# All right-hand SBUF pools moved down by 128 bytes: where weights and moving operands lie modulo 256

## The chip, the cores and the metric

The kernel runs on one core of one Trainium2 chip. The metric is the device time of that core in microseconds. The time before is the median of three runs, 2258.73 us (2254.85 to 2258.97). Beside it there is one profiled execution, whose trace all rows here come from.

## The reference, cut to what matters

One residual decoder block over a sequence of 2048 positions with 1024 channels, all in float32. The normalized and modulated input `h` is multiplied by a wide weight `w_in` (1024 x 8192). Its columns feed a recurrent branch and a branch of windowed attention; both are projected, gated, merged and projected once more.

```python
h = rms_norm(x, g_norm[l]) * (1.0 + scale[:, None, :]) + shift[:, None, :]
proj = h @ w_in[l]
x_rnn, z_rnn, q, k, v, z_attn, g_r, g_a = jnp.split(proj, IN_SPLITS, axis=-1)
...
y_rnn = (hr * jax.nn.silu(z_rnn.astype(jnp.float32))).astype(dt) @ w_out_rnn[l]
...
y_attn = (o * jax.nn.silu(z_attn.astype(jnp.float32))).astype(dt) @ w_out_attn[l]
...
merged = jax.nn.sigmoid(g_r + bg_r) * y_rnn + jax.nn.sigmoid(g_a + bg_a) * y_attn
x = x + gate[:, None, :] * (merged @ w_o[l])
return rms_norm(x, g_final)
```

## The kernel before, in words

**Precision.** Every large product is made of three matmuls of type float32r: each operand is split into a high and a low part, and `mm3` (line 151) issues high x high, high x low and low x high into one accumulator. In a matmul the *weights* (`lhsT`, 128 x 128) are loaded into the array by a weight load, and the *moving operand* (the right operand, 128 x up to 512) streams past them. The weight load of the next matmul runs while a matmul streams.

**Block products.** The products of `h` with the columns of `w_in` (other than the value columns) are done in seven block multiplications instead of eight for each pair of column blocks (`strassen`, line 348). One block multiplication is one call of `prod`: four slices `k` with three matmuls each, twelve matmuls of 512 columns. The weights are the S tiles (`s_tile`, line 190): a ring of seven tiles S0 to S6 of 4096 bytes per partition, each with the high part of four 128 x 128 blocks and then the low part. The moving operands are the tiles T (`slot`, line 485), of 8192 bytes per partition, four slices of 2048 bytes; they hold blocks of `h` and sums of them, named B11, B21, B22, T1 to T4. The kernel runs over the sequence in two halves `f`. In the first, S is made on the core: raw columns are loaded by SyncE's queue into the R tiles, ScalarE makes the high part and GpSimd the low part (`split_s`, line 207), and each S is also stored to memory. In the second half the S tiles are loaded back (`load_next`, line 312). Outputs go to the PSUM tiles X, Y, Z, W and V.

**Value products.** Ahead of the block products of each half stands `values` (line 797). Here the roles are turned: S moves, 256 columns at a time, and slices of T, or of the tile b12 (line 553), are the weights.

**Attention and output products.** Then comes the attention stage. Between its steps a generator (`steps`) issues the output products `pj`: weights in S0 to S3 again (`load_wd`, line 335), moving operands `yh` and `yl` (`split_y`, line 1688). The last stage multiplies by `w_o` into `pq`, with the weights `mh`, `ml` and the moving operands `oh`, `ol`.

**Where the tiles lie.** On-chip memory is filled from two sides in each partition. The left side grows upward, the right side downward from byte 229,344. `pS`, `pR`, `wS` and `wq` are opened on the right in this order, and after `wS` and `wq` are closed `fl` takes their place. The left side holds the pool `hp` of the T tiles, `vx` with b12, and later `ap` and `fp`. All sizes here are multiples of 32 bytes, and a slice of 128 float32 values is 512 bytes. The start addresses in the kernel before, in bytes within a partition, are:

| tile | pool, side | start | modulo 256 | modulo 512 |
|---|---|---|---|---|
| S0 to S3 | pS, right | 212,960 + 4096 i | 224 | 480 |
| S4, S5, S6 | wS, right | 192,480; 196,576; 200,672 | 224 | 480 |
| yh; yl | fl, right | 159,712 + 2048 i; 178,144 + 2048 i | 224 | 480 |
| T | hp, left | 18,528 + 8192 i | 96 | 96 |
| b12 high, low, first half | vx, left | 149,248; 157,440 | 0 | 256 |
| b12 high, low, second half | vx, left | 141,536; 149,728 | 224 | 224 |
| oh; ol | fp, left | 18,528; 51,296 | 96 | 96 |
| mh; ml | fp, left | 108,640 + 4096 i; 120,928 + 4096 i | 96 | 96 |

The pool `vx` is opened twice, and b12 lies in another place in each half. Every slice of S, T, yh, yl, oh, ol, mh, ml and b12 begins at a multiple of 512 bytes behind the start of its tile.

The pools and the helper of the change stand in this part of the kernel:

Of the kernel before, what the change touches and what calls it, by code (L numbers as in the profile page):

```python
# [10 lines left out]
F32 = mybir.dt.float32  # L11
# [9 lines left out]
P = 128  # L21
# [68 lines left out]
def decoder_block(ctx, tc, x, c, positions, g_norm, w_mod, b_mod, w_in, b_gate, conv_w, conv_b,  # L90
# [4 lines left out]
    def T(pool, shape, dt, tag, **kw):  # L95
        cnt[0] += 1
        return pool.tile(shape, dt, tag=tag, name=f"{tag}_{cnt[0]}", **kw)
# [388 lines left out]
        return T(hp, [P, KH, CH], F32R, "T", bufs=14)  # L486


    pS = pools.open("pS", side="right", bufs=1)
    pR = pools.open("pR", side="right", bufs=1)  # L490
    wS = pools.open("wS", side="right", bufs=1)
# [1403 lines left out]
```

## Time and profile before

| | |
|---|---|
| median of three runs | 2258.73 us (2254.85 to 2258.97) |
| span of the profiled execution | 2256.2 us |
| TensorE busy | 2212.2 us, 98% of the span |
| share of TensorE in the chain that ended last | 58% |
| mean granted TensorE clock | 0.992 |
| read from memory, written to it | 357.44 MB, 213.91 MB |

The profiled execution's own time is known by its span, 2256.2 us, which lies inside the spread of the three runs. The stages by the span: start and first values to 138 us, block products of the first half to 700 us, values of the second half to 813 us, its block products to 1386 us, attention with most of the output products to about 2005 us, and the rest of these with the last stage to the end.

How to read the rows: a row of the timeline gives the start in us, the time from the first start to the last end, the engine, the line and operation, the output and inputs by the program's names, the shape and the number of instructions merged. Line 149 is `mm`, the helper that issues every matmul, so the tiles tell matmuls apart. The end of a matmul is modelled and reaches into the next one; the starts are measured, and the spacing of matmuls is the difference of starts.

### The profile page before, as it was taken

How to read it: one execution, taken by the hardware profiler on the slowest of the kernel's cores; microseconds unless marked ns; L12 is line 12 of the kernel's file. 1: busy time of each engine (PE TensorE's matmuls, PEld its weight loads, DVE VectorE, ACT ScalarE, POOL GpSimd, SP SyncE). 2: the span in 40 equal slices, each digit the busy share in tenths (PEclk: the TensorE clock that was granted, in tenths of full speed). 3: DMA queues.
4: the chain of work that ended last, by engine and by line, in shares of the span. 5: the costliest groups of instructions: out<-in, count | busy, mean ns of one | idle time of the engine just before them, and what ended most of it. 6: DMA issues, size and time to landing. Idle time of an engine off the chain costs nothing.

```text
span 2256.2 us, 33998 instructions
## 1 busy us (share of the span) xinstructions
PE 2212.2 (98%) x11422; PEld 1856.8 (82%) x11422; DVE 1346.9 (60%) x2380; ACT 1257.3 (56%) x2481; POOL 977.8 (43%) x734
## 2 busy tenths in 40 slices
PE   8999999999999999999999999999999998999998
PEld 5988888888878988888888877888889887978887
DVE  5838877778555815444445343566667877666443
ACT  6638668668543627556546302677778887533211
POOL 2457676767557422222223102455566655332100
PEclk9999999999999999999999999999999999999999
DMA  8367887887998378888888988988888897899442
GB/s 286 115 219 255 281 290 260 291 277 262 326 277 292 110 235 267 278 279 272 283 280 278 332 291 277 287 252 256 263 269 262 241 264 217 255 329 285 153 132 89
DMA packets 428626, 573.64 MB, mean 254 GB/s; under 512 B 72134, under 2 KB 292514, under 8 KB 427428
## 3 DMA queue, kind: packets, MB, share of 16 engines
q1 hardware_dynamic: 390612, 451.73, 64.9%
q10 hardware_dynamic: 37648, 119.70, 13.8%
q8 instruction: 90, 1.47, 0.3%
q14 instruction: 84, 0.69, 0.1%
q0 software_dynamic: 192, 0.05, 0.0%
HBM read 357.44 MB, written 213.91 MB: 253 GB/s over the span
## 4 chain that ended last, share of the span: by engine, by line
PE 58%; DMA 4%; DVE 2%; issue 2%; ACT 2%; POOL 2%; SPq 1%; ACTq 0%; POOLq 0%; DVEq 0%
PE pj L149 11%; PE X L149 9%; PE V L149 8%; PE pq L149 8%; PE Z L149 4%; PE W L149 4%; PE sc L149 4%; PE Y L149 4%; PE o L149 4%; DMA vraw<-vN 1%; PE pT L1498 1%; PE pg L149 1%; DMA meT<-fg 1%; PE pT L1511 1%; DMA kraw<-qT 1%
## 5 line engine op out<-in xcount | busy, mean ns | idle before, releaser
L149 PE MATMUL pj<-yh,S 128*128 128x512 f32 x1024 | 370.0, 405 | 10.5 <-ACT yh L157 4.6
L149 PE MATMUL V<-T,S 128*128 128x512 f32 x1344 | 330.8, 395 | 1.7 <-DVE t L450 1.7
L149 PE MATMUL X<-T,S 128*128 128x512 f32 x1344 | 331.3, 395 | 0.9 <-POOL S L163 0.9
L163 POOL TENSOR_TENSOR S<-R,S 128x512 fp32r<-128x512 f32 x168 | 253.5, 1516 | 171.6 <-ACT S L157 70.3
L149 PEld LDWEIGHTS V<-T,S 128*128 128x128 f32 x1344 | 252.6, 188 | 61.9 <-DVE t L450 2.3
L149 PEld LDWEIGHTS X<-T,S 128*128 128x128 f32 x1344 | 252.4, 188 | 61.2 <-POOL S L163 1.7
L149 PEld LDWEIGHTS pj<-yh,S 128*128 128x128 f32 x1024 | 194.3, 190 | 49.4 <-ACT yh L157 6.1
L149 PE MATMUL pj<-yl,S 128*128 128x512 f32 x512 | 202.9, 396 | 6.1 <-POOL yl L163 5.1
L1414 ACT ACTIVATE pp<-pp,st 128x256 f32<-128x256 f32 (+3 forms) x256 | 133.8, 524 | 95.8 <-DVE st L1413 94.8
L163 POOL TENSOR_TENSOR S<-s,S 128x512 fp32r<-128x512 f32 x84 | 128.6, 1531 | 121.7 <-ACT S L157 77.8
L149 PE MATMUL Z<-T,S 128*128 128x512 f32 x672 | 165.8, 395 | 0.0
L149 PE MATMUL Y<-T,S 128*128 128x512 f32 x672 | 165.7, 395 | 0.0
L149 PE MATMUL W<-T,S 128*128 128x512 f32 x672 | 165.4, 395 | 0.0
L149 PEld LDWEIGHTS W<-T,S 128*128 128x128 f32 x672 | 126.3, 188 | 30.1 <-issue 0.9
L149 PEld LDWEIGHTS Z<-T,S 128*128 128x128 f32 x672 | 126.3, 188 | 29.4
L149 PEld LDWEIGHTS Y<-T,S 128*128 128x128 f32 x672 | 126.4, 188 | 29.2
L166 DVE TENSOR_TENSOR ptl<-pT,pth 128x384 fp32r<-128x384 f32 (+1 forms) x160 | 97.9, 628 | 75.6 <-ACT pth L157 73.4
L163 POOL TENSOR_TENSOR s<-R,s 128x512 fp32r<-128x512 f32 x32 | 46.5, 1452 | 204.9 <-ACT s L157 201.8
L157 ACT ACTIVATE S<-R 128x512 fp32r<-128x512 f32 x168 | 101.8, 622 | 47.4 <-DMA R<-in_w_in_dram 21.6
L905 DVE SCALAR_TENSOR_TENSOR xc<-xr,par,xc 128x512 f32<-128x512 f32 x96 | 95.6, 996 | 47.3 <-ACT xc L899 45.0
L1478 ACT ACTIVATE pp<-pp,M 128x256 f32<-128x256 f32 (+3 forms) x256 | 117.9, 522 | 10.0 <-DVE M L1601 10.0
L1413 DVE CUSTOM_DVE_ANT_0 pp<-sc,msk 128x256 f32<-128x256 f32 (+3 forms) x256 | 104.7, 449 | 24.6 <-PE sc L149 22.1
(334 smaller groups left out, 4729.9 us busy)
## 6 DMA issues: line engine op xcount, KB each, us to landing
sD<-S ACTq DMA_DIRECT2D x196, 512.0 KB, 4.1
S<-sD SPq DMA_DIRECT2D x196, 512.0 KB, 4.9
S<-wD SPq DMA_DIRECT2D x100, 512.0 KB, 5.7
R<-in_w_in_dram SPq DMA_DIRECT2D x136, 256.0 KB, 4.3
wD<-s ACTq DMA_DIRECT2D x64, 256.0 KB, 5.1
T<-in_w_mod_dram SPq DMA_DIRECT2D x8, 1024.0 KB, 12.0
vN<-ev SPq DMA_DIRECT2D x64, 128.0 KB, 2.8
zaT<-ev SPq DMA_DIRECT2D x32, 256.0 KB, 4.1
```

The costliest lines, as they stand in the source:

```text
L149: nc.tensor.matmul(o, lhsT=l, rhs=r, start=st, stop=sp, **kw)
L157: nc.scalar.activation(o, i, AF.Copy)
L163: nc.gpsimd.tensor_tensor(o, i, h.bitcast(F32), ALU.subtract)
L166: return nc.vector.tensor_tensor(o, i, h.bitcast(F32), ALU.subtract).ins
L905: nc.vector.scalar_tensor_tensor(xc, xr[:, i : i + CH], cw(i), xc, ALU.mult, ALU.add)
L1413: nc.vector.tensor_tensor_reduce(pdst, s_ps, mask, 1.0, 3e38, ALU.add, ALU.min, m_)
L1414: nc.scalar.activation(pdst, pdst, AF.Exp, bias=m_, scale=-1.0, accum_out=l_)
L1478: nc.scalar.activation(pp, pp, AF.Copy, scale=w)
L1498: nc.tensor.transpose(pt[:, c0 + j * P : c0 + (j + 1) * P], pp[i][:, k * P : (k + 1) * P], ident)
L1511: nc.tensor.transpose(pt[:, c * P : (c + 1) * P], pp[:, half * P : (half + 1) * P], ident)
```

## The change

A pool `shift` of one tile, 128 bytes per partition (32 float32 values), is opened on the right side ahead of all others and stays open to the end. Nothing writes or reads its tile. Every right-hand pool behind it starts 128 bytes lower: S, yh and yl at 96 modulo 256 (352 modulo 512). The left-hand pools stay where they are.

```diff
@@ -486,6 +486,8 @@
         return T(hp, [P, KH, CH], F32R, "T", bufs=14)
 
 
+    shift = ctx.enter_context(tc.tile_pool(name="shift", bufs=1, side="right"))
+    T(shift, [P, 32], F32, "shift")
     pS = pools.open("pS", side="right", bufs=1)
     pR = pools.open("pR", side="right", bufs=1)
     wS = pools.open("wS", side="right", bufs=1)
```

## The prediction

> **What bounds the kernel now.** I read the page first (busy shares and the chain that ended last), then the groups of matmul instructions, then the timeline of TensorE, where the start times of neighbouring groups give the spacing of matmuls.
>
> ```profile
> span 2256.2 us, 33998 instructions
> PE 2212.2 (98%) x11422; PEld 1856.8 (82%) x11422; DVE 1346.9 (60%) x2380; ACT 1257.3 (56%) x2481; POOL 977.8 (43%) x734
> ...
> PE 58%; DMA 4%; DVE 2%; issue 2%; ACT 2%; POOL 2%; SPq 1%; ACTq 0%; POOLq 0%; DVEq 0%
> ```
>
> TensorE is busy 98% of the span and has 58% of the chain; no other engine has more than 2%. Which matmuls fill it, and whether they wait, stands in the groups:
>
> ```profile
> L149 PE MATMUL pj<-yh,S 128*128 128x512 f32 x1024 | 370.0, 405 | 10.5 <-ACT yh L157 4.6 <-DMA S<-wD 2.5 <-ACT S L157 1.8
> L149 PE MATMUL X<-T,S 128*128 128x512 f32 x1344 | 331.3, 395 | 0.9 <-POOL S L163 0.9
> L149 PE MATMUL V<-T,S 128*128 128x512 f32 x1344 | 330.8, 395 | 1.7 <-DVE t L450 1.7
> ...
> L149 PE MATMUL Z<-T,S 128*128 128x512 f32 x672 | 165.8, 395 | 0.0
> L149 PE MATMUL Y<-T,S 128*128 128x512 f32 x672 | 165.7, 395 | 0.0
> L149 PE MATMUL W<-T,S 128*128 128x512 f32 x672 | 165.4, 395 | 0.0
> ```
>
> The block products (moving operand T, weights S) are 1344 + 1344 + 3 x 672 = 4704 matmuls of 512 columns, and they waited 0.9 + 1.7 = 2.6 us in all. So in these stages nothing but the spacing of the matmuls sets the time. The "mean ns" of a matmul (395) is longer than the spacing, because one overlaps the next; the spacing has to be read from starts.
>
> **The spacing now.** The timeline of TensorE inside the block products, 72 matmuls in a row without a wait:
>
> ```profile
> 1239.15 2.96 PE L149 MATMUL X<-T,S 128*128 128x512 f32 x12
> 1241.94 2.95 PE L149 MATMUL Y<-T,S 128*128 128x512 f32 x12
> 1244.73 2.94 PE L149 MATMUL X<-T,S 128*128 128x512 f32 x12
> 1247.51 2.95 PE L149 MATMUL V<-T,S 128*128 128x512 f32 x12
> 1250.30 2.96 PE L149 MATMUL Z<-T,S 128*128 128x512 f32 x12
> 1253.10 2.95 PE L149 MATMUL W<-T,S 128*128 128x512 f32 x12
> 1255.89 2.48 PE L149 MATMUL V<-T,S 128*128 128x512 f32 x10
> ```
>
> (1255.89 - 1239.15) / 72 = 232.5 ns. Now the output products of the attention stage. They read weights of the same pool (tiles S0 to S3) with the same order of three matmuls, also 512 columns, but their moving operands yh and yl lie in a right-hand pool:
>
> ```profile
> 1388.58 0.39 PE L149 MATMUL pj<-yl,S 128*128 128x512 f32 x1
> 1388.81 0.61 PE L149 MATMUL pj<-yh,S 128*128 128x512 f32 x2
> ...
> 1396.06 0.39 PE L149 MATMUL pj<-yl,S 128*128 128x512 f32 x1
> ```
>
> From the first row to the last are eleven times three matmuls: (1396.06 - 1388.58) / 33 = 226.7 ns. The last stage has both operands in the left-hand pool fp:
>
> ```profile
> 2160.67 0.39 PE L149 MATMUL pq<-oh,mh 128*128 128x512 f32 x1
> 2160.90 0.39 PE L149 MATMUL pq<-ol,mh 128*128 128x512 f32 x1
> ...
> 2165.43 0.39 PE L149 MATMUL pq<-oh,mh 128*128 128x512 f32 x1
> ```
>
> Seven times three matmuls: (2165.43 - 2160.67) / 21 = 226.7 ns again. In the layout of the kernel before, every S, yh and yl starts at 224 modulo 256 and every T, oh, mh at 96. So weights and moving operand at (224, 224) and at (96, 96) go at 226.7 ns, and only the block products at (224, 96) at 232.5 ns. The moving address alone does not order these three (96 is in the slow and in a quick one), nor does the weights' (224 likewise); being alike does.
>
> **A second pair of rows for it, with one size held.** In the value products the tiles change roles: S moves (256 columns) and T or b12 is the weight. The pool of b12 is opened twice: in the first half of the kernel b12 lies at 0, in the second at 224 modulo 256, each against S at 224.
>
> ```profile
> 116.00 0.40 PE L149 MATMUL Z<-S,b12h 128*128 128x256 f32 x2
> ...
> 118.84 0.40 PE L149 MATMUL W<-S,b12h 128*128 128x256 f32 x2
> ...
> 782.05 0.40 PE L149 MATMUL Z<-S,b12h 128*128 128x256 f32 x2
> ...
> 784.93 3.01 PE L149 MATMUL X<-S,T 128*128 128x256 f32 x24
> 787.77 3.01 PE L149 MATMUL Z<-S,T 128*128 128x256 f32 x24
> 790.62 0.40 PE L149 MATMUL W<-S,b12h 128*128 128x256 f32 x2
> ```
>
> Twenty-four matmuls each. First half, unlike: 2.84 us, 118.3 ns. Second half, alike: 2.88 us, 120.0 ns. With T as weight (unlike by 128): (790.62 - 784.93) / 48 = 118.5 ns. The same program text changes its spacing with the address alone. This pair tells two more things. Here S and b12 are 256 apart modulo 512 (S at 480, b12 at 224), and that still counts as alike. This matters, because after the change S lies at 352 and T at 96 modulo 512, also 256 apart, while (224, 224) and (96, 96) above are alike modulo 512 too. And at 256 columns the alike state is the slower one, by 1.5 ns.
>
> **What the change does, part by part.** It reserves 128 bytes at the top of the right side; nothing reads or writes them, so no instruction, wait or transfer is added. S moves from 224 to 96 modulo 256 and meets T at 96.
>
> Block products: 4704 x (232.5 - 226.7) ns = 27.3 us less. I take off 3%, 0.8 us, for the few matmuls after each interruption (in the rows of 1388 the steady spacing begins at the fifth one), so 26.5. Bounds: nothing, if 512 columns do not follow the rule, and 27.3.
>
> Value products: at most 1152 matmuls with T as weight (456 + 240 + 240 + 216 in the rows below) become alike and go from 118.5 to 120.0 ns: 1.7 us more. In the second half 192 have b12 as weight (by the program 48 for each of four column groups m); they become unlike, 0.3 us less. Net +1.4.
>
> ```profile
> L149 PE MATMUL X<-S,T 128*128 128x256 f32 x456 | 59.8, 284 | 0.0
> ...
> L149 PE MATMUL V<-S,T 128*128 128x256 f32 x240 | 31.4, 284 | 0.0
> L149 PE MATMUL Z<-S,T 128*128 128x256 f32 x240 | 30.9, 282 | 0.0
> ...
> L149 PE MATMUL W<-S,T 128*128 128x256 f32 x216 | 28.2, 283 | 0.0
> ```
>
> Output products of the attention stage: S and yh, yl move together, from 224 to 96, and stay alike: nothing. The last stage has left-hand operands only: nothing.
>
> What hides less when TensorE is quicker: in the block products the other work must keep up with a rate 2.5% higher.
>
> ```profile
> GB/s 286 115 219 255 281 290 260 291 277 262 326 277 292 110 235 267 278 279 272 283 280 278 332 291 277 287 252 256 263 269 262 241 264 217 255 329 285 153 132 89
> ...
> 138.00:700.00 562.00, 559.42 (x2421) 452.29 (x2419) 414.01 (x459) 360.01 (x578) 379.72 (x254) 1.00 0.82 279
> ...
> 813.00:1386.00 573.00, 573.00 (x2472) 462.54 (x2471) 258.84 (x358) 271.07 (x413) 131.19 (x99) 1.00 0.86 283
> ...
> 1236.00:1350.00 114.00, 114.00 (x493) 92.42 (x492) 1.00 0.93 310
> ```
>
> The first line is the page's GB/s in forty slices. The others are rows by stage; after the length come the busy times of PE, PEld, DVE, ACT and POOL (of PE and PEld alone in the third), then granted clock, DMA share and GB/s. In the first half the busiest helper is VectorE with 414 of 562 us, and 74% goes to 76%. DMA goes from 283 to 290 GB/s in the second half, and from 310 to 318 in its densest 114 us, where TensorE now has no gap at all; one slice of the page reached 332 GB/s. I take 0.6 us for small new waits.
>
> Sum: -26.5 + 1.4 + 0.6 = -24.5 us. The profiled execution then has 2256.2 - 24.5 = 2231.7 us. The median of the runs shown is 2.5 us above that execution's span (2258.73), so the forecast is 2258.7 - 24.5 = 2234.2, said as 2234.
>
> **The skill against the rows.** The spacings 226.7 and 232.5 above differ between address relations. The Trainium skill, TensorE: Matmul & The Clock Gate, section Part 2 (What happens when you issue a matmul), says that the array has two independent read ports, so that loading the next weights takes no read bandwidth from the running matmul; SBUF — State Buffer, section Who interferes with whom, says that TensorE never waits on anyone. By these the address could not matter and the sum would be 0; the b12 rows, 118.3 against 120.0 ns, disagree. The first page's spacing for 512 columns, 512 / 2.4 + 2.5 = 215.8 ns, is also below both spacings here.
>
> **The rivals.**
> *No change, 2258.7.* The block products differ from the others in something else than the address (where they accumulate, what runs beside them), or the unread tile takes no space. For it: the rows of 512 columns compare different stages. Against it: pj at 1388 runs right behind the last block product with the same weight pool, and b12 changes its spacing with its address alone. Chance 0.07. The pages' rule of independent ports stands on this side.
> *Another limit takes over, 2247.* DMA at 93% in the densest stretch cannot go faster, and the second half, about half of the 26.5 us, gains nothing: 2234 + 13 = 2247. Against it: no matmul of that half waits today, and 318 GB/s is below the 332 reached. Chance 0.05.
> *Slower, 2267.* At 256 columns the alike state costs 1.5 ns more. If the distance of 256 modulo 512 gives that sign at 512 columns too, the block products pay 4704 x 1.5 ns = 7.1 us, with the 1.4 of the values 8.5 us. It decides from a spacing of 233.2 ns on (0.7 ns x 4704 + 1.4 = 4.5 us, 0.2% of the time, about what a measurement of this kernel can tell from no change). Against it: both alike relations of 512 columns gain, and where both the relation of 256 apart and 256 columns are at hand, the spacing is the alike one. Chance 0.06.
>
> **How the numbers follow.** Forecast 0.82, no change 0.07, another limit 0.05, slower 0.06. Beside the unknown waits, the stretches of half clock can fall otherwise once the later stages come 25 us earlier:
>
> ```profile
> 1460.10:1466.90 6.80, 6.18 (x24) 0.50 0.80 250
> 1555.70:1562.40 6.70, 5.19 (x21) 0.50 0.56 208
> 1890.20:1897.00 6.80, 5.81 (x20) 0.50 0.40 144
> ```
>
> Each costs up to half its length, 3.4 us; two more or two fewer are 7 us. That makes 2227 to 2241 about the forecast; I add 1 us below for the whole 27.3, and reach up past the other limit: 2226 to 2248. Faster by over 0.2%: 0.82 + 0.05 = 0.87; within: 0.07; slower: 0.06.
>
> **What would show it.** In the changed kernel's timeline twelve block matmuls should take 2.72 us from start to start where they take 2.79 now, and the 24 value matmuls with T 2.88 where they take 2.84; the rows of pj and pq should keep 226.7 ns. The counts of instructions should be those of before. The forecast is wrong if the block products keep 232.5 ns, or if they go at 226.7 and new idle time stands before them, with DMA or POOL as releaser.

## The result and the profile after

| | before | changed |
|---|---|---|
| median | 2258.15 us (2254.85 to 2258.97, 4 runs) | 2240.82 us (2236.96 to 2242.47, 4 runs) |
| span of the profiled execution | 2256.2 us | 2235.2 us |
| ratio of the runs, 95% interval | | 0.9918 [0.9902, 0.9934] |

The change makes the kernel 17.3 us faster. The forecast was 2234.0 us, in a range from 2226 to 2248, by a gain of 24.5 us. The sign, the cause and the range hold; a part of the gain is missing. Repeated on another chip, the same kernel took 2235.36 us beside 2257.96 us, 22.6 us less (ratio 0.9902 [0.9884, 0.992]). The two intervals overlap, so whether the missing part differs between chips is not shown.

The page of the changed kernel, with its first lines, its chain and its groups of block products (busy us, mean ns of one, then the idle time just before them and what ended it):

```profile
span 2235.2 us, 33998 instructions
PE 2185.0 (98%) x11422; PEld 1851.0 (83%) x11422; DVE 1350.6 (60%) x2380; ACT 1256.1 (56%) x2481; POOL 983.4 (44%) x734
...
PE 55%; DMA 7%; issue 3%; POOL 2%; DVE 2%; SPq 2%; ACT 2%; ACTq 0%; POOLq 0%; DVEq 0%
...
L149 PE MATMUL X<-T,S 128*128 128x512 f32 x1344 | 324.5, 390 | 4.4 <-POOL S L163 3.8
L149 PE MATMUL V<-T,S 128*128 128x512 f32 x1344 | 324.5, 390 | 3.3 <-DVE t L450 3.0
...
L149 PE MATMUL Z<-T,S 128*128 128x512 f32 x672 | 161.9, 390 | 0.0
L149 PE MATMUL Y<-T,S 128*128 128x512 f32 x672 | 161.8, 390 | 0.0
L149 PE MATMUL W<-T,S 128*128 128x512 f32 x672 | 161.7, 389 | 0.0
```

Every count of instructions is that of before. The five groups lost busy time; added up, 1159.0 us became 1134.4. Two of them, X and V, gained idle time: 0.9 + 1.7 us became 4.4 + 3.3 us. The chain shows the same from its side, since DMA has 7% of it where it had 4%. The prediction looked at the engines alone there, 2% at most, and passed over that 4%.

TensorE's timeline inside the block products of the second half (start, time to the last modelled end, then the instructions merged in the row):

```profile
1225.78 2.88 PE L149 MATMUL X<-T,S 128*128 128x512 f32 x12
1228.50 2.88 PE L149 MATMUL Y<-T,S 128*128 128x512 f32 x12
...
1242.10 1.07 PE L149 MATMUL V<-T,S 128*128 128x512 f32 x4
```

Twelve matmuls take 2.72 us from start to start, and the 72 from the first row to the last (1242.10 - 1225.78) / 72 = 226.7 ns. It was 232.5.

The value products with T as weight, and the output products of the attention stage, in the timeline of the same kernel:

```profile
780.49 3.04 PE L149 MATMUL X<-S,T 128*128 128x256 f32 x24
783.37 3.04 PE L149 MATMUL Z<-S,T 128*128 128x256 f32 x24
...
1376.05 0.39 PE L149 MATMUL pj<-yl,S 128*128 128x512 f32 x1
...
1381.49 0.39 PE L149 MATMUL pj<-yl,S 128*128 128x512 f32 x1
```

The first two are 2.88 us apart, 120.0 ns a matmul (it was 118.5). The last two are eight times three matmuls apart, 5.44 us / 24 = 226.7 ns, as before.

**Where the time went.** Landmarks are the starts, in the timeline, of the first matmul of each kind and, at the end of each half's block products, of their last.

| part | before | changed | difference | changed, on the other chip |
|---|---|---|---|---|
| start to the first block product | 138.7 | 140.2 | +1.4 | 139.5 |
| block products, first half | 578.0 | 571.5 | -6.5 | 569.6 |
| values, second half | 96.8 | 97.5 | +0.7 | 97.3 |
| block products, second half | 572.8 | 560.5 | -12.3 | 560.0 |
| from the end of these to the first pq | 618.9 | 615.0 | -3.9 | 616.0 |
| the rest | 251.0 | 250.5 | -0.4 | 251.3 |

Each half has 2352 matmuls of block products. Over all intervals under 300 ns their mean spacing fell from 232.42 to 227.07 ns; times 2352 this makes 12.6 us for each half. The second half gained that, the first only half of it.

### The profile page after: what moved, and what is told of

Same layout as the page of the kernel before. It is cut to its first block, busy times and chain, and to the rows that moved or that the text cites. A ratio compares the mean times of both kernels' runs of the same rounds, so it can differ in the third digit from the quotient of the medians.

```text
span 2235.2 us, 33998 instructions
## 1 busy us (share of the span) xinstructions
PE 2185.0 (98%) x11422; PEld 1851.0 (83%) x11422; DVE 1350.6 (60%) x2380; ACT 1256.1 (56%) x2481; POOL 983.4 (44%) x734
## 4 chain that ended last, share of the span: by engine, by line
PE 55%; DMA 7%; issue 3%; POOL 2%; DVE 2%; SPq 2%; ACT 2%; ACTq 0%; POOLq 0%; DVEq 0%
PE pj L149 12%; PE X L149 8%; PE pq L149 8%; PE V L149 7%; PE W L149 4%; PE Z L149 4%; PE sc L149 3%; PE Y L149 3%; PE o L149 3%; DMA R<-in_w_in_dram 2%; PE pg L149 1%; DMA S<-wD 1%; PE pT L1500 1%; DMA vraw<-vN 1%; PE pT L1513 1%
## 5 line engine op out<-in xcount | busy, mean ns | idle before, releaser
L163 POOL TENSOR_TENSOR S<-R,S 128x512 fp32r<-128x512 f32 x168 | 257.8, 1542 | 170.9 <-ACT S L157 75.3
L149 PE MATMUL X<-T,S 128*128 128x512 f32 x1344 | 324.5, 390 | 4.4 <-POOL S L163 3.8
L149 PE MATMUL V<-T,S 128*128 128x512 f32 x1344 | 324.5, 390 | 3.3 <-DVE t L450 3.0
L163 POOL TENSOR_TENSOR S<-s,S 128x512 fp32r<-128x512 f32 x84 | 128.5, 1530 | 112.3 <-ACT S L157 70.2
L163 POOL TENSOR_TENSOR s<-R,s 128x512 fp32r<-128x512 f32 x32 | 45.3, 1416 | 203.7 <-ACT s L157 169.1
L1480 ACT ACTIVATE pp<-pp,M 128x256 f32<-128x256 f32 (+3 forms) x256 | 117.9, 522 | 10.0 <-DVE M L1603 10.0
```

What stands on the lines that cost most here:

```text
L149: nc.tensor.matmul(o, lhsT=l, rhs=r, start=st, stop=sp, **kw)
L163: nc.gpsimd.tensor_tensor(o, i, h.bitcast(F32), ALU.subtract)
L1480: nc.scalar.activation(pp, pp, AF.Copy, scale=w)
```

## The experiments

All were run beside the kernel before on the same chip. A distance below is the number of bytes by which the weights start behind the moving operand, modulo 256. Before, the block products are at 128 and the value products with T as weight at 128 as well; in the changed kernel both are at 0.

**A reserve of 64 bytes.** S goes to 160, T stays at 96.

```diff
-    T(shift, [P, 32], F32, "shift")
+    T(shift, [P, 16], F32, "shift")
```

> The reserved tile is 64 bytes instead of 128: S lies at 160 modulo 256, T at 96, unlike by 64. Theory A (weights and moving operand have to be alike modulo 256): the block products keep an uneven spacing of 228 to 234 ns, 2.74 to 2.81 us for twelve, and the time stays within 8 us of before. Rival B (any move of the right-hand pools, or the reserved tile as such, brings the gain): 226.7 to 227.1 ns, 2.72 us for twelve, and the time of the changed kernel. Output products pj stay alike and at 226.7 in both.

One run took 2252.87 us (before on this chip: median 2260.13, 2255.55 to 2261.58). The timeline of this kernel:

```profile
1242.20 2.96 PE L149 MATMUL X<-T,S 128*128 128x512 f32 x12
1245.00 2.96 PE L149 MATMUL V<-T,S 128*128 128x512 f32 x12
```

Twelve take 2.80 us, 233.3 ns: no gain in the block products, so moving the pools is not enough, and theory B falls. That the whole time is nevertheless lower comes from elsewhere. The values of the second half took 93.5 us where they took 96.8, since at their new distances (192 with T, 64 with b12) the 256-column matmuls go at 115.9 and 113.4 ns in the mean, and the attention stage was 4.4 us shorter. The block products of the second half took 1.9 us more. This is one run, so its total is not used for more.

The mean of 115.9 ns hides two steady spacings. These are four rows of the values with T in the second half of this kernel, all at the same distance of 192:

```profile
757.56 2.99 PE L149 MATMUL W<-S,T 128*128 128x256 f32 x24
760.39 2.99 PE L149 MATMUL Z<-S,T 128*128 128x256 f32 x24
...
771.49 2.88 PE L149 MATMUL X<-S,T 128*128 128x256 f32 x24
774.21 2.88 PE L149 MATMUL V<-S,T 128*128 128x256 f32 x24
```

The first two are 2.83 us apart, 117.9 ns a matmul, and the last two 2.72 us, 113.3 ns. In the first half, where b12 lies at a distance of 96, the values with T keep 117.8 ns throughout; in the second they keep 113.3 once the first b12 products, at 64, have run (a stretch of 39 at 749 us goes at 113.3 as well). So the distance alone does not always fix the spacing. That what ran just before matters too would fit, but is not shown.

**A reserve of 256 bytes.** S moves, but keeps its old relation to T. To make room, one of four small buffers of the start is left out.

```diff
-    T(shift, [P, 32], F32, "shift")
+    T(shift, [P, 64], F32, "shift")
...
-        accs[j, q] = acc = T(vx, [P, 256], F32, "acc", bufs=4)
+        accs[j, q] = acc = T(vx, [P, 256], F32, "acc", bufs=3)
```

> The reserved tile is 256 bytes: every right-hand address is another one than before, but S is at 224 modulo 256 again and T at 96. To make room one accumulator buffer of the first stage is left out. Theory A: the block products are back at 232.4 ns, 2.79 us for twelve, value products with T back at 118.6 ns, and the time at 2255 to 2262. Rival B (reserved tile, or lower addresses as such): 226.7 to 227.1 ns and about 2240.

One run took 2262.83 us. Its timeline:

```profile
1244.15 2.96 PE L149 MATMUL X<-T,S 128*128 128x512 f32 x12
1246.94 2.95 PE L149 MATMUL Y<-T,S 128*128 128x512 f32 x12
```

2.79 us for twelve, the spacing of before. Neither the move nor the reserve does anything of its own.

**The left side moved instead.** In the kernel before, the 128 bytes are reserved on the left ahead of all other pools, so that T goes up to meet S at 224 and the right side stays.

```diff
+    shift = ctx.enter_context(tc.tile_pool(name="shift", bufs=1))
+    T(shift, [P, 32], F32, "shift")
```

> The 128 bytes are reserved on the left side instead: T goes to 224 modulo 256 and meets S, which stays at 224. Theory A: the block products go to 226.7 to 227.1 ns as in the changed kernel, and the time to 2236 to 2244. Rival C (96 is a good place for S, or 224 a bad one): the spacing stays at 232.4 ns and the time near 2258.

The median was 2240.85 us, ratio 0.9918 [0.9902, 0.9935], which is the ratio of the change itself. The timeline of this kernel (its lines stand two further down):

```profile
1242.51 2.88 PE L151 MATMUL V<-T,S 128*128 128x512 f32 x12
1245.23 2.88 PE L151 MATMUL X<-T,S 128*128 128x512 f32 x12
```

2.72 us again. Which side moves makes no difference, and theory C falls: not S at 96 but S and T alike.

**The spacing by itself.** A kernel of nothing but groups of 96 matmuls, in which the weights' distance changes from group to group: 0, 128, 4, 16, 32, 64, 96, 160, 192, 224, 252, 256, 0, 128 at 512 columns, then 0, 128, 32, 64, 96, 160, 192, 224 at 256 columns, then 0, 128, 64, 32 in bfloat16.

```python
a = (i % 8) * P + d // size
b = (i % 3) * 512
nc.tensor.matmul(t[:, :n], lhsT=w[:, a : a + P], rhs=m[:, b : b + n], start=i == 0, stop=i == N - 1)
```

> None of the block's computation: only groups of 96 matmuls with a new weight load for each and nothing else on the chip, the weights starting 0 to 256 bytes behind the moving operand modulo 256. Theory A: at 512 columns of float32r 226.7 ns at 0 and at 256, and 228 to 234 ns at most other distances; at 256 columns 120.0 ns at 0 and about 118.5 at others. Which of the small distances (4, 16, 32) still count as alike is open; from the b12 rows 32 does not at 256 columns. Rival D (the spacing comes from what the other engines and the DMA do beside the block products): all distances at 226.7 here. For bfloat16 no trace has a row; if the two operand reads meet in the same way, an uneven spacing shows there too.

Its timeline, one row a group (the output's letter only counts the groups):

```profile
32.95 22.48 PE L59 MATMUL b<-M,W 128*128 128x512 f32 x96
55.26 22.47 PE L59 MATMUL c<-M,W 128*128 128x512 f32 x96
...
277.53 21.93 PE L59 MATMUL e<-M,W 128*128 128x512 f32 x96
299.29 22.48 PE L59 MATMUL f<-M,W 128*128 128x512 f32 x96
...
321.61 11.67 PE L59 MATMUL a<-M,W 128*128 128x256 f32 x96
333.12 11.55 PE L59 MATMUL b<-M,W 128*128 128x256 f32 x96
...
412.42 20.89 PE L59 MATMUL a<-Mb,Wb 128*128 128x512 bf16 x96
433.15 20.88 PE L59 MATMUL b<-Mb,Wb 128*128 128x512 bf16 x96
453.87 20.88 PE L59 MATMUL c<-Mb,Wb 128*128 128x512 bf16 x96
```

At a distance of 128: (55.26 - 32.95) / 96 = 232.4 ns. At 0: (299.29 - 277.53) / 96 = 226.7. With nothing else running on the core, these are the kernel's two spacings, and rival D falls. At 256 columns and distance 0 it is (333.12 - 321.61) / 96 = 119.9, the kernel's 120.0. In bfloat16 it is (433.15 - 412.42) / 96 = 215.9 at 0 and 215.8 at 128, no difference.

Other distances repeat what the kernels showed. 512 columns at 64 give 233.4 (the 64-byte reserve: 233.3). 256 columns at 192 give 117.8, one of the two spacings of the 64-byte reserve. 256 columns at 32 and at 160 give 118.3 and 120.0: b12 of the first half was at 32 before and is at 160 now, and went from 118.3 to 120.0, as its rows in the changed kernel show, 24 matmuls in 2.88 us:

```profile
117.15 0.40 PE L149 MATMUL Z<-S,b12h 128*128 128x256 f32 x2
...
120.03 0.40 PE L149 MATMUL W<-S,b12h 128*128 128x256 f32 x2
```

**The changed kernel on another chip.** No edit, more rounds.

> The changed kernel once more, to see how much of the difference between its profiled execution (21 us below that of before) and its median (17.3 below) is spread. Theory: the spacing of the block products is the same in every execution (226.7 to 227.1 ns), the median is 2238 to 2243, and executions differ by the stretches of half clock in the attention stage and by waits of the first half between 570 and 690 us, some 2 to 5 us.

The median was 2235.36 us (2233.22 to 2240.92), ratio 0.9902 [0.9884, 0.992], below the 2238 to 2243 that were expected; the spacing was 227.06 ns, as on the first chip. The waits for V and X within 560 to 708 us (waiting engine and tile, then the releaser; us in all, times, longest), first of the changed kernel on the first chip, then of this run:

```profile
PE X L149 <- POOL S L163: 3.8, 2, 2.8
PE V L149 <- DVE t L450: 3.0, 2, 2.7
PE X L149 <- ACT u L383: 0.6, 2, 0.4
```

```profile
PE V L149 <- DVE t L450: 2.1, 2, 1.8
PE X L149 <- POOL S L163: 1.3, 2, 1.0
PE X L149 <- ACT u L383: 1.3, 3, 0.6
```

All lie in the last products of the first half. The spacing repeats; the waits do not. The next experiments look for what they wait on.

**Wide loads of the last columns.** S L163 is the low part made by GpSimd, which follows a load of raw columns. The columns of q and k come in narrow pieces; here they are loaded as whole runs of 128 columns. The results are of other columns. The same edit was made in the kernel before.

```diff
-            yield (base, "rotated"), [wcol(base + hh * P, 32) for hh in range(H)]
+            yield (base, "rotated"), [wcol(base, 2 * P)]
...
-        return [wcol(base + r0, n) for pc in cuts[t : t + 2] for _, r0, n in pc]
+        return [wcol(base + t * P, 2 * P)]
```

> The changed kernel with the raw columns of the rotated and plain query and key products taken as whole runs of 128 columns instead of pieces of 32 to 96, so other columns than the reference's are multiplied; as many bytes, fewer and longer descriptors and fewer DMA issues. Theory W (the gain that is missing in the first half went into new waits because the narrow loads of the last products there cannot be brought faster): the waits of the first half between 570 and 690 us, 9 us in the changed kernel, fall to under 3 us, and the time to 2230 to 2235. Rival V (the waits come from GpSimd's or VectorE's own pace): they stay, and the time stays within 2 us of the changed kernel's.

> The kernel before with the same whole runs of 128 columns (again other columns than the reference's). Theory W: its waits there, 4 us, mostly go, the time falls by 2 to 5 us, and the difference between this kernel and the changed one with whole runs is the whole gain of the alike addresses, 22 to 26 us. Rival V: no change against before, and a difference of 17 us as without whole runs.

The changed kernel took 2235.56 us (0.9904 [0.9886, 0.9921]), the same as without the edit (2235.36); the one before 2257.21 us (0.9995 [0.9986, 1.0005]). In the changed kernel, intervals over 300 ns between block products fell from 8.6 to 4.4 us in excess, but the lost time stands at the head of the next values instead (waits of the wide kernel, 560 to 760 us):

```profile
PE pg L526 <- DVE hf L543: 2.7, 1, 2.7
PE X L149 <- ACT T L536: 1.3, 1, 1.3
```

Theory W falls: the number of pieces moves the waits and doesn't remove them. The two wide kernels are 21.7 us apart, close to the 22.6 without the edit, and not the 17 that theory V expected, which had come from the first chip.

**Operands made one product earlier.**

```diff
-    LEAD = 4
+    LEAD = 5
```

> The changed kernel with every step that makes an S (loads, splits, stores) five products ahead instead of four. Theory W': the supply of S is late by its latency, and one product (2.7 us) of more lead covers part of the new waits: 2 to 5 us less than the changed kernel. Rival: the supply is short of rate, or the ring of seven S is full, and a lead changes nothing or costs waits: within 2 us, or slower.

2249.6 us, ratio 0.9964 [0.9951, 0.9977], 14 us slower than the changed kernel on the same chip. The excess of the intervals over 300 ns in the first half rose to 19.4 us. Some 4.6 us of it are not waits: at 255, 589 and 668 us the granted clock was 0.50 for 3.4 us each, beside waits of 1.9 to 4.0 us, where the changed kernel's block products had 1.00 throughout on both chips. Starting earlier makes the waits longer, so W' falls; which buffer or transfer is short with the longer lead was not followed up.

**Every distance.** The kernel of single groups again, with 64 float32r matmuls at each distance from 0 to 252 in steps of 4, first at 512 and then at 256 columns.

```diff
-WIDE = (0, 128, 4, 16, 32, 64, 96, 160, 192, 224, 252, 256, 0, 128)
+WIDE = tuple(range(0, 256, 4))
```

> None of the block's computation: groups of 64 matmuls of float32r as in the run before, at every distance from 0 to 252 bytes in steps of 4, first with 512 columns, then with 256. Theory A' (a distance sets a fixed rhythm of weight load and stream; 0 and 252 are at 226.7 ns with 512 columns): each group has one spacing or a short repeating pattern, all between 220 and 236 ns at 512 columns and between 113 and 121 at 256, with the same value wherever a distance was measured before (128: 232.4 and 118.7; 64: 233.4 and 113.3; 192: 228.9 and 117.8). Open: whether a distance beats 0 at 512 columns, and whether one distance d and its counterpart 256 - d are good for both sizes, which is what the kernel would need. Rival: the values depend on the group before, then the same distance comes out otherwise than in the run before.

Its timeline at the distances 120 and 124, then at 204 and 208:

```profile
457.67 14.69 PE L59 MATMUL g<-M,W 128*128 128x512 f32 x64
472.20 14.98 PE L59 MATMUL h<-M,W 128*128 128x512 f32 x64
...
769.04 14.67 PE L59 MATMUL d<-M,W 128*128 128x512 f32 x64
783.55 15.00 PE L59 MATMUL e<-M,W 128*128 128x512 f32 x64
```

From the first row to the second are 14.53 us / 64 = 227.0 ns, the change of group included, and from the third to the fourth 14.51 / 64 = 226.7. Inside the groups the mean is 226.7 ns at 0, 120, 132, 144, 156, 204, 228 and 252, 228.3 at 240 and 228.8 at 192. At all others it is 229.9 to 237.7. So being alike is enough for the quick spacing, but it is not the only distance that has it. At 256 columns it is 113.3 ns at 52, 64, 76 and 88, 120.0 at 0, and from 115.6 to 122.3 elsewhere. The highest are a little above the 236 and 121 that were expected. Some distances did not repeat: 128 gave 233.4 ns here and 232.4 in the groups of 96, and at 256 columns 120.0 against 118.7. The distances 0, 64 and 192 repeated at both widths. Together with the 113.3 and 117.9 ns of the 64-byte reserve, one distance can thus have more than one spacing, and the rival that a group depends on what ran before it is not excluded.

**Without most of the stores of S.** In the first half each S is also stored, and the waits lie where that traffic is densest. Here only the first 140 are stored, in the changed kernel and in the one before; the loads of the second half keep their number and sizes.

```diff
-                nc.scalar.dma_start(sD[k], t2[:].bitcast(F32))
+                if k < 140:
+                    nc.scalar.dma_start(sD[k], t2[:].bitcast(F32))
...
-            nc.sync.dma_start(t[:].bitcast(F32), sD[n])
+            nc.sync.dma_start(t[:].bitcast(F32), sD[n % 140])
```

> The changed kernel without the stores of the last 56 S tiles of the first half (28 MB of DMA traffic from about 540 to 700 us); the second half loads earlier ones in their place, so its last products are others than the reference's. Theory X (the new waits of the first half are DMA's rate: the transfers of the last products there fill the 16 engines): the waits between T matmuls of the first half, 8.6 to 10.4 us in the changed kernel, fall to under 4 us, also those at the start of the next values, and the time falls by 4 to 8 us to 2228 to 2236. Rival (the order and latency of the steps, not the rate): waits and time stay within 2 us of the changed kernel.

> The kernel before without the same stores. Theory X: its waits, 4.7 us, go to about 1, the time falls by 2 to 5 us, and the difference to the changed kernel without the stores is the whole gain of the spacing, 23 to 26 us. Rival: no change against before.

The changed kernel took 2227.44 us (0.9862 [0.9843, 0.9881]), the one before 2251.55 us (0.9966 [0.9952, 0.9979]): 24.1 us apart, against 24.5 forecast; the intervals of the two ratios leave several microseconds of room on either side. Both fell by more than was expected: the one before by 7.5 us, where 2 to 5 were; the changed one by some 9 to 13, where 4 to 8 were. The second figure is an estimate from its ratios on the other two chips, 0.9918 and 0.9902, since with its stores it was not run on this one. Rows of the stretch 560 to 708 us (length; busy PE, PEld, DVE, ACT, POOL; clock, DMA share, GB/s) of the kernel before, the changed one, and the changed one without the stores:

```profile
560.00:708.00 148.00, 145.42 (x635) 116.76 (x635) 87.47 (x116) 65.62 (x109) 92.28 (x64) 1.00 0.94 304
```

```profile
560.00:708.00 148.00, 140.34 (x625) 113.77 (x623) 83.78 (x114) 64.92 (x105) 88.04 (x62) 1.00 0.93 297
```

```profile
560.00:708.00 148.00, 147.50 (x677) 122.14 (x676) 95.13 (x122) 70.02 (x114) 95.79 (x68) 1.00 0.59 153
```

In the first two DMA is at 0.94 and 0.93, and quicker matmuls did not get more through in 148 us: 635 and 625. In the third DMA is at 0.59, TensorE is idle for 0.5 us, and 677 matmuls run. These windows are fixed in time, so they do not hold quite the same work; the last 672 block matmuls of the half, which do, took 165.0 us before, 167.7 and 165.8 in the changed kernel on its two chips, and 157.8 in the changed kernel without the stores. There the whole first half took 561.6 us, nearly the 559.9 of the second, and the excess of its intervals over 300 ns was 1.9 us instead of 8.6 to 10.4.

So the stores at the end of the first half are what ate the gain there: with them the excess rose by 4.0 to 5.8 us from the kernel before to the changed one, and without them by 1.1. That they do it by the rate of the transfers, as theory X says, fits the DMA share and the loads of raw columns, which land later beside the stores (KB each, then median us from issue to landing, in 560 to 708 us of the changed kernel and of the one without the stores):

```profile
R<-in_w_in_dram SPq DMA_DIRECT2D x41, 64.0 KB, 4.5
...
R<-in_w_in_dram SPq DMA_DIRECT2D x42, 64.0 KB, 3.1
```

But the edit also frees the S tiles that a store holds until it has landed, and takes the issues of the stores from ScalarE's queue. No run separates these. In the changed kernel's trace ScalarE and GpSimd waited 0.7 us for a store to land when they wrote an S between 560 and 712 us, and 17.0 us for raw columns, which speaks for the rate.

**The next half's input loaded later.** If transfers are what is short there, one can be put off: the load of the next half's rows of x, with its norm, comes ten products later. Nothing is left out.

```diff
-        xs = load_x(xp, 2, "x", 2)
+        xs = []
...
+        later(10, lambda: xs.extend(load_x(xp, 2, "x", 2)))
...
-            later(5 + r, lambda r=r: square(r))
+            later(15 + r, lambda r=r: square(r))
```

> The changed kernel with the load of the next half's x (two transfers of 1 MB) and its norm put ten products later, away from the tables' loads at the start of the rotated products; the results are the reference's. If the waits at 575 to 612 us come from that heap of transfers: 2 to 4 us less than the changed kernel, and the fastest version. If the traffic is only moved: within 1 us of it.

2241.13 us, ratio 0.9922 [0.9908, 0.9936]: no better than the changed kernel. Its waits in 560 to 708 us:

```profile
PE X L149 <- ACT u L383: 7.5, 4, 3.6
```

The waits for V and for S are gone, and ScalarE's evictions u come late instead. ScalarE has the norm's work beside them, but it also stood idle for 1.87 us right before the first late one, so that the norm's work makes them late is not shown. Behind two of these waits TensorE then ran at half clock:

```profile
639.89 4.58 PE L149 MATMUL X<-T,S 128*128 128x512 f32 x12 [2.75 <-ACT u L383]
644.31 2.89 PE L149 MATMUL Y<-T,S 128*128 128x512 f32 x12
```

From start to start these twelve took 4.42 us where others take 2.72, with a granted clock of 0.50 from 639.9 to 643.3 us. The same happened from 663.8 to 670.6 us, and both together cost 4.7 us of this execution. No version tried with the whole computation beats the changed kernel.

## Why the prediction was right, and where it was off

**Spacing of the block products, -26.5: right in kind, 1.3 us too much.** Alike operands go at 226.7 ns in long runs, as read from pj, pq and b12 before the change. Over all intervals under 300 ns the mean fell by 5.35 ns, not 5.8: 4704 x 5.35 = 25.2 us. Part of this is the allowance for the matmuls after an interruption, which should have been some 8% and not 3%. The distance of 256 modulo 512, from which a slower rival was made, counts as alike; that rival falls.

**Value products, +1.4: right, in part by luck.** The spacing with T as weight is 120.0 ns in long runs as forecast, and the values of the second half took 0.7 us more, half of the 1.4 for both halves. Over all its matmuls it rose by 1.2 and not 1.5 ns, 1.4 us instead of 1.7. That b12 of the first half would slow down as well, 192 x 1.7 ns = 0.3 us, was not seen: it went from one unlike distance to another. The two errors cancel.

**pj and pq, nothing: right.** Both keep 226.7 ns in long runs.

**Small new waits, +0.6: the mis-sized term.** In the groups of X and V the idle time rose by 7.7 - 2.6 = 5.1 us. By the intervals over 300 ns, the excess in the first half rose from 4.6 to 10.4 us on the first chip and to 8.6 on the second, 5.8 and 4.0 us where 0.6 was allowed. This is the prediction's own sign of being wrong, new idle time before the block products with GpSimd (POOL) as a releaser, in a small size. The prediction had DMA at 0.82 over the first half and at 0.93 in the densest stretch of the second, and took the second for the tight one. It was the other way round: the second half gained 12.3 us, all but 0.3 of its 12.6, while the first half's last 150 us, already at 0.94 before, hide behind that half's mean. So the rival of another limit was right in its mechanism and wrong in its place, and its size was a part of the 13 us. In the changed kernel the stores of S took about half of the transfer time there: 46.0% of the 16 DMA engines' time between 560 and 708 us, beside 46.8% for the other loads and stores.

**Sum.** In the trace: -25.2 of spacing, +5.8 of waits, +1.4 of values make -18.0 us. The two spans differ by 21.0, and the 3.0 us between lie mostly in the attention stage, which was 3.9 us shorter. The median lost 17.3; it is less than the 21.0 of the spans because the profiled execution of the changed kernel was the fastest of its four, 2236.96 us. The prediction allowed several microseconds there for stretches at half clock, and the changed kernel's are shorter (windows of the three; PEclk 0.50 is the third number from the end):

```profile
1446.00:1449.40 3.40, 3.40 (x16) 3.23 (x15) 2.42 (x12) 1.88 (x6) 0.00 (x0) 0.50 0.60 223
...
1541.60:1545.00 3.40, 3.40 (x15) 3.11 (x15) 1.70 (x9) 2.61 (x10) 1.97 (x2) 0.50 0.12 43
...
1872.70:1876.10 3.40, 3.11 (x13) 2.92 (x13) 1.73 (x3) 0.00 (x0) 3.27 (x3) 0.50 0.41 142
```

Three of 3.4 us where there were three of 6.7 to 6.8; half of the difference is 5.1 us, more than the stage lost. In the run on the other chip they were as long as before, and the stage was 2.9 us shorter all the same. So the half-clock stretches do not settle the 3.9 us; what does stays open. It need not be the change: the versions of the kernel before with wide loads and without the stores, whose addresses are those of before, took 616.1 and 615.8 us there, 2.8 and 3.1 us less than the kernel before itself.

**The pages against the rows.** The independent read ports of the Trainium skill, TensorE: Matmul & The Clock Gate, section Part 2, would have made the change worth nothing. The single groups disagree for float32r (226.7 against 232.4 ns, address alone). The rule that TensorE never waits on anyone, in the Trainium skill, SBUF — State Buffer, section Who interferes with whom, is said there of what other engines do; it does not speak of TensorE's own two operands, so the prediction read too much out of it. The spacing of 215.8 ns which the Trainium skill, TensorE: Matmul & The Clock Gate, section Part 2, gives for 512 columns agrees with the bfloat16 groups, 215.8 ns at every distance tried.

## What to carry to other kernels

The spacing of matmuls is read from starts in long runs without a wait, and two stages that issue the same shape at different spacings are a reason to compare the addresses of their operands. In a kernel of float32r matmuls, put weights and moving operand at the same address modulo 256 where 512 columns stream, and try it at 256 columns before keeping it, since there it cost 1.2 ns a matmul in the mean. Before a gain is booked for a quicker bottleneck, look at the DMA share in the last stretch of each stage and not in its mean: the stretch at 0.94 here gave back 4 to 6 of 25 us.

## What was not expected of the hardware

- In float32r, 512 columns go at 226.7 ns at eight of 64 distances, and at up to 237.7 at the others; at 256 columns the range is 113.3 to 122.3 ns, and alike operands are among the slower. In bfloat16 the distances 0, 128, 64 and 32 all gave 215.8 ns. What in the chip makes these rhythms is not shown by any run here.
- A distance can have more than one steady spacing (128 at 512 columns: 232.4 and 233.4 ns in two kernels; 192 at 256 columns: 117.9 and 113.3 ns within one execution).
- A wait of 2 to 4 us inside the block products is in some executions followed by 3.4 or 6.8 us at a granted clock of 0.50 (operands one product earlier, input loaded later), and in others not (2.7 and 2.8 us in the changed kernel).
- At a distance of 204 the block products would keep 226.7 ns, and the value products with T, then at 52, would go at 113.3: by these figures 1152 x 6.7 ns = 7.7 us less than the changed kernel, an estimate that was not tried, and one that takes each distance to keep its one spacing, which 192 did not.
